# A streaming-encoder trunk on one core: SBUF places of matmul operands, and the piece size of the weight split

## Chip, cores and metric

The kernel runs on one core of a Trainium2 chip. The metric is device time in microseconds (us), the median of the runs. A second number, the span, is the time from the first to the last instruction in the one execution that was profiled.

## What is computed

Two identical layers are applied to 256 tokens of width 2048, all in float32. Biases, the rotary tables and the masks are left out here.

```python
def reference(x, ...):
    x = layer_norm(x, ln_in_g, ln_in_b)
    for l in range(DEPTH):                       # 2 layers
        h = x @ w_in[l]                          # 2048 -> 512 + 256 + 64 + 4 * 1024
        c_q, c_kv, k_rope, rq, rk, rv, rg = split_columns(h)
        a = mla_group(...)                       # 8 heads, softmax, low-rank q and kv
        r = retention_group(...)                 # 4 heads, decayed scores, group norm, gate
        mix = jnp.concatenate([a, r], axis=-1) @ w_out[l]           # 2048 -> 2048
        x = layer_norm(ALPHA * x + mix, ln1_g[l], ln1_b[l])
        f = (jax.nn.silu(x @ w_gate[l]) * (x @ w_up[l])) @ w_down[l]  # 2048 -> 5632 -> 2048
        x = layer_norm(ALPHA * x + f, ln2_g[l], ln2_b[l])
    return x
```

## The kernel before

**Numbers in two parts.** Each operand of a large matmul is held as two tiles of type float32r, a rounded part `hi` and the rest `lo`. The function `split` makes them: ScalarE casts the source into `hi` (line 250), and VectorE subtracts `hi` from the source into `lo` (line 251). A product takes three matmuls for each 128 rows of the contraction, called a triple below: hi by hi, hi by lo, lo by hi.

**Which operand is loaded and which is streamed.** TensorE loads 128 columns of one operand as its stationary operand (a weight load, PEld in the profile) and then streams the other one, the moving operand. There are two arrangements.
- `mm_x` (lines 238 to 240) and the function `mm` of the Strassen blocks (lines 804 to 806) load 128 tokens of the activations (`xTh`, `xTl`, `hTh`, `hTl`, `sfh`, `sfl`, `mixAh` and others) and stream 512 columns of the weights (320 in the block `ckv`).
- `mm_w` (lines 245 to 247) loads 128 columns of the weights and streams 256 tokens of the activations.

**Weights.** All weights lie in HBM as a stream of blocks, in the order of `PLAN` and `UNITS`. A block is at most 2048 columns on 128 partitions (1 MB). The class `Weights` walks through the stream. SP's queue loads a block into one of three `raw` buffers, up to three blocks ahead of the split. `_prep` splits one block into one of three `hi` and one of three `lo` buffers, and `done`, called after the last matmul on a block, frees its buffers and calls `_prep` for the block three places later. A plain block (kind "std") is split in two halves, so there are two casts and two subtractions. The blocks of the Strassen scheme (kinds B11, T1, B21, T2, T3, T4, B22) are split in one piece of 2048 columns already, some of them after VectorE has added two raw blocks (line 187).

**Amount of work for each layer.** There are 80 plain blocks of 4 by 512 columns that two token halves stream (24 matmuls each), 48 more matmuls of 512 columns in `pr` and `pv`, and ten Strassen chunks of 180 matmuls of 512 columns each. Of those 180, 48 load `sfh` or `sfl` (the outputs `sY`, `sZ` and part of `sW`); the others load `xTh` or `xTl`. `mm_w` has 1296 matmuls of 256 columns in a layer, and `ckv` has 96 of 320 columns.

**Order of work.** The order of instructions on each engine is fixed when the program is built. At the end of the attention part, and at the end of the feed-forward part of the first layer, `chunk_tail` keeps three weight blocks and finishes token half 0 before token half 1, so that the layer norm of half 0 (`Norm.apply`, lines 277 to 285, on VectorE, then transposes on TensorE and a split into `xTh` and `xTl`) runs beside the matmuls of half 1. `chunk_head` of the next part begins with half 0 in the same way. There are three such handovers. While they last, the splits of the next weight blocks and the layer norm share VectorE and ScalarE.

**Where the tiles lie.** SBUF is filled from the bottom by pools, one behind the other: `const`, `wraw`, `wspl`, `small`, and then `att` or the pools of the feed-forward part. Tiles begin at multiples of 32 bytes. Two unused tiles, `pad0` and `pad1`, and a third, `pad2`, shift what lies behind them. Modulo 256 bytes, in the program as built, the operands begin here (before the change):

```
res, xTh, xTl                                      128
raw, hi, lo                                        192
sfh, sfl                                           192
hTh, hTl                                           128
cqTh, cqTl, ckT, mixAh, mixAl, mixRh, mixRl        128
qT, kT, vt, rv (float32 attention operands)        128
ident                                               96
```

All steps inside these tiles from one operand of a matmul to the next are multiples of 256 bytes. So in `mm_x`, `mm` and `mm_w` the stationary and the moving operand stand at distance 64 modulo 256 (in one direction or the other), except for the matmuls on `sfh` and `sfl`, where the distance to `hi` and `lo` is 0. The distance is that of the addresses along the free dimension of a partition.

Of the kernel before, what the change touches and what calls it, by code (L numbers as in the profile page):

```python
# [10 lines left out]
F32 = mybir.dt.float32  # L11
# [7 lines left out]
P = 128  # L19
# [92 lines left out]
def trunk(ctx: ExitStack, tc: tile.TileContext, x, pos, w, lnp, cols, eye, consts, out):  # L112
# [3 lines left out]
    const = ctx.enter_context(tc.tile_pool(name="const", bufs=1))  # L116
    wraw = ctx.enter_context(tc.tile_pool(name="wraw", bufs=3))
    wspl = ctx.enter_context(tc.tile_pool(name="wspl", bufs=3))
    small = ctx.enter_context(tc.tile_pool(name="small", bufs=6))
    psp = ctx.enter_context(tc.tile_pool(name="psp", bufs=8, space=PSUM))  # L120

    res = const.tile([P, 2, D], F32, name="res")
    xTh = const.tile([P, KD, S], F32R, name="xTh")
    xTl = const.tile([P, KD, S], F32R, name="xTl")
# [5 lines left out]
    mhalf = const.tile([P, 8], F32, name="mhalf")  # L130

    ident = const.tile([P, P], F32, name="ident")
    const.tile([P, 88], F32, name="pad0")

    def bank(tag_name):
        return psp.tile([P, 512], F32, tag="ps", name=tag_name)
# [1 line left out]
    class Weights:  # L138
# [26 lines left out]
        def _prep(self):  # L165
            i = self.n_prep
            if i >= len(UNITS):
                return
            self.loads(i + 1)
            hi = wspl.tile([P, 2048], F32R, tag="hi", name=f"hi{i}")  # L170
            lo = wspl.tile([P, 2048], F32R, tag="lo", name=f"lo{i}")
            kind, b = UNITS[i]
            if kind == "std":
                n = SIZES[b]
                raw = self.raw.pop(b)
                for a, e in ((0, n // 2), (n // 2, n)):
                    split(hi[:, a:e], lo[:, a:e], raw[:, a:e])
            else:
                r = {j: self.raw.get(b[j]) for j in b}
                into, frm = {"B11": ("11", None), "B21": ("21", None), "B22": ("22", None), "T1": ("11", "12"),  # L180
                             "T2": ("11", "22"), "T4": ("11", "21"), "T3": ("12", "22")}[kind]
                if frm is not None:
                    if kind in STRASSEN_ADD_BY_DMA:
                        j = b[frm]
                        G.dma_start(r[into], w[OFFS[j]:OFFS[j + 1]].rearrange("(p n) -> p n", p=P), accum_op=ALU.add)
                    else:
                        V.tensor_tensor(r[into], r[into], r[frm], ALU.add)  # L187
                split(hi, lo, r[into])
                for j in {"T4": ("11", "21"), "T3": ("12",), "B22": ("22",)}.get(kind, ()):
                    self.raw.pop(b[j])  # L190
            self.hi[i], self.lo[i] = hi, lo
            self.n_prep += 1
            self.loads(i + 4)
# [55 lines left out]
    def split(hi, lo, src):  # L249
        A.copy(hi, src)  # L250
        V.tensor_tensor(lo, src, hi.bitcast(F32), ALU.subtract)  # L251
# [169 lines left out]
    for l in range(DEPTH):  # L421
# [317 lines left out]
        ffp = ff_ctx.enter_context(tc.tile_pool(name=f"ff{l}", bufs=1))  # L739
        W.rpool = ff_ctx.enter_context(tc.tile_pool(name=f"rs{l}", bufs=3))  # L740
        normf = Norm(f"f{l}")
        ffp.tile([P, 16], F32, tag="pad", name="pad1")
        sfh = ffp.tile([P, 4, 4, P], F32R, tag="sfh", name="sfh")
        sfl = ffp.tile([P, 4, 4, P], F32R, tag="sfl", name="sfl")

# [123 lines left out]
            hprev.append((0, c, v2))  # L869
            hprev.append((1, c, v5))  # L870

        ffp.tile([P, 48], F32, tag="pad2", name="pad2")
        for f0, f1 in FF_PARTS:
            nk = 4 * (f1 - f0)
            hTh = ffp.tile([P, 12, S], F32R, tag="hTh", name="hTh")
# [136 lines left out]
```

## Time and profile before

| what | us |
|---|---|
| median of 3 runs | 2206.98 |
| lowest and highest of them | 2205.0, 2208.04 |
| the profiled execution's own time | 2205.94 |
| its span | 2204.1 |
| TensorE busy | 2170.3 |
| VectorE busy | 1590.1 |
| ScalarE busy | 1024.4 |

The profiled execution is 1.04 us faster than the median. Its own time holds 1.84 us that lie outside the span. The granted clock of TensorE has a mean of 0.998 of full speed. The busy time of TensorE is a sum over instructions whose ends are modelled, so the pace of the matmuls is read from their starts.

### The profile page before, as it was taken

How to read it: one execution, taken by the hardware profiler on the slowest of the kernel's cores; microseconds unless marked ns; L12 is line 12 of the kernel's file. 1: busy time of each engine (PE TensorE's matmuls, PEld its weight loads, DVE VectorE, ACT ScalarE, POOL GpSimd, SP SyncE). 2: the span in 40 equal slices, each digit the busy share in tenths (PEclk: the TensorE clock that was granted, in tenths of full speed). 3: DMA queues.
4: the chain of work that ended last, by engine and by line, in shares of the span. 5: the costliest groups of instructions: out<-in, count | busy, mean ns of one | idle time of the engine just before them, and what ended most of it. 6: DMA issues, size and time to landing. Idle time of an engine off the chain costs nothing.

```text
span 2204.1 us, 26848 instructions
## 1 busy us (share of the span) xinstructions
PE 2170.3 (98%) x11084; PEld 1838.2 (83%) x11084; DVE 1590.1 (72%) x1687; ACT 1024.4 (46%) x1089; POOL 35.5 (2%) x46
## 2 busy tenths in 40 slices
PE   6999999999999999999999999999999999999997
PEld 5988988788888888888889899878888888888886
DVE  8565675887698578788675656667967885877976
ACT  4554333455455345455344543335544553545552
POOL 0000000000000000000000000000000000000000
PEclk9999999999999999999999999999999999999999
DMA  7544455566567557476555444555665674565653
GB/s 258 210 156 153 173 203 179 211 209 229 172 228 253 205 193 245 161 259 195 190 196 178 151 168 167 204 188 191 225 235 188 231 243 166 200 250 208 210 210 115
DMA packets 63467, 441.22 MB, mean 200 GB/s; under 512 B 7408, under 2 KB 7664, under 8 KB 11504
## 3 DMA queue, kind: packets, MB, share of 16 engines
q1 hardware_dynamic: 60048, 418.46, 52.0%
q0 software_dynamic: 2880, 20.97, 5.2%
q8 instruction: 87, 1.43, 0.3%
q14 instruction: 36, 0.29, 0.0%
q10 hardware_dynamic: 416, 0.07, 0.0%
HBM read 437.38 MB, written 2.10 MB: 199 GB/s over the span
## 4 chain that ended last, share of the span: by engine, by line
PE 48%; DVE 2%; issue 0%; ACT 0%; DVEq 0%; ACTq 0%
PE db L238 4%; PE db L240 4%; PE db L239 4%; PE sX L805 2%; PE sX L804 2%; PE sW L805 2%; PE sW L804 2%; PE sX L806 2%; PE sW L806 2%; PE prq L246 1%; PE prq L247 1%; PE prq L245 1%; PE sQ L805 1%; PE sQ L804 1%; PE sQ L806 1%; PE wo L239 1%
## 5 line engine op out<-in xcount | busy, mean ns | idle before, releaser
L251 DVE TENSOR_TENSOR lo<-raw,hi 128x1024 fp32r<-128x1024 f32 (+3 forms) x754 | 1033.5, 1407 | 418.9 <-ACT hi L250 417.0
L250 ACT CAST hi<-raw 128x1024 fp32r<-128x1024 f32 (+3 forms) x754 | 874.7, 1199 | 990.4 <-PE db L240 298.6
L238 PE MATMUL db<-hi,hTh 128*128 128x512 f32 x704 | 278.2, 395 | 0.0
L239 PE MATMUL db<-lo,hTh 128*128 128x512 f32 x704 | 275.3, 391 | 0.0
L240 PE MATMUL db<-hi,hTl 128*128 128x512 f32 x704 | 272.6, 391 | 0.0
L238 PEld LDWEIGHTS db<-hi,hTh 128*128 128x128 f32 x704 | 132.2, 188 | 31.0 <-ACT hTh L250 3.7
L240 PEld LDWEIGHTS db<-hi,hTl 128*128 128x128 f32 x704 | 132.1, 188 | 30.3
L239 PEld LDWEIGHTS db<-lo,hTh 128*128 128x128 f32 x704 | 132.3, 188 | 27.4
L245 PE MATMUL prq<-xTh,hi 128*128 128x256 f32 x512 | 144.0, 281 | 0.0
L246 PE MATMUL prq<-xTl,hi 128*128 128x256 f32 x512 | 142.6, 279 | 0.0
L247 PE MATMUL prq<-xTh,lo 128*128 128x256 f32 x512 | 142.6, 279 | 0.0
L187 DVE TENSOR_TENSOR raw<-raw,raw 128x2048 f32<-128x2048 f32 x60 | 137.1, 2285 | 0.5
L805 PE MATMUL sX<-lo,xTh 128*128 128x512 f32 x320 | 125.9, 394 | 0.0
L804 PE MATMUL sX<-hi,xTh 128*128 128x512 f32 x320 | 125.5, 392 | 0.0
L806 PE MATMUL sX<-hi,xTl 128*128 128x512 f32 x320 | 124.5, 389 | 0.0
L245 PEld LDWEIGHTS prq<-xTh,hi 128*128 128x128 f32 x512 | 97.2, 190 | 0.1
L246 PEld LDWEIGHTS prq<-xTl,hi 128*128 128x128 f32 x512 | 96.2, 188 | 0.1
L247 PEld LDWEIGHTS prq<-xTh,lo 128*128 128x128 f32 x512 | 96.1, 188 | 0.0
L805 PE MATMUL sQ<-lo,xTh 128*128 128x512 f32 x240 | 94.5, 394 | 0.0
L804 PE MATMUL sQ<-hi,xTh 128*128 128x512 f32 x240 | 94.1, 392 | 0.0
L806 PE MATMUL sQ<-hi,xTl 128*128 128x512 f32 x240 | 93.2, 388 | 0.0
L691 DVE SCALAR_TENSOR_TENSOR res<-res,db 128x512 f32<-128x512 f32 x64 | 43.8, 684 | 67.7 <-PE db L240 67.7
(265 smaller groups left out, 3974.7 us busy)
## 6 DMA issues: line engine op xcount, KB each, us to landing
raw<-w SPq DMA_DIRECT2D x377, 1024.0 KB, 4.9
raw<-w POOLq DMA_DIRECT2D x20, 1024.0 KB, 8.4
raw<-w SPq DMA_DIRECT2D x8, 640.0 KB, 3.9
lng<-lnp SPq DMA_DIRECT2D x4, 1024.0 KB, 4.9
lnb<-lnp SPq DMA_DIRECT2D x4, 1024.0 KB, 5.8
res<-x SPq DMA_DIRECT2D x4, 512.0 KB, 6.4
out<-res SPq DMA_DIRECT2D x8, 256.0 KB, 2.6
cst<-consts SPq DMA_DIRECT2D x2, 976.5 KB, 8.2
```

The source lines that it names most:

```text
L187: V.tensor_tensor(r[into], r[into], r[frm], ALU.add)
L238: PE.matmul(ps[:, :ncol], sh, wh[:, k, :ncol], start=first and k == 0, stop=False)
L239: PE.matmul(ps[:, :ncol], sh, wl[:, k, :ncol], start=False, stop=False)
L240: PE.matmul(ps[:, :ncol], sl, wh[:, k, :ncol], start=False, stop=last and k == nk - 1)
L245: PE.matmul(ps_ap, wh[:, k, c0:c0 + P], xh[:, k, :], start=k == 0, stop=False)
L246: PE.matmul(ps_ap, wh[:, k, c0:c0 + P], xl[:, k, :], start=False, stop=False)
L247: PE.matmul(ps_ap, wl[:, k, c0:c0 + P], xh[:, k, :], start=False, stop=k == nk - 1)
L250: A.copy(hi, src)
L251: V.tensor_tensor(lo, src, hi.bitcast(F32), ALU.subtract)
L804: PE.matmul(ps, a, wh[:, k, :], start=first and k == 0, stop=False, skip_group_check=True)
L805: PE.matmul(ps, a, wl[:, k, :], start=False, stop=False, skip_group_check=True)
L806: PE.matmul(ps, b, wh[:, k, :], start=False, stop=k == 3, skip_group_check=True)
```

## The change

Two things are changed. `pad0` shrinks by 16 float32 elements (64 bytes), and an unused tile of 64 bytes is placed first in `small`; `pad1` and `pad2` go. With that `raw`, `hi` and `lo` move 64 bytes down, to 128 modulo 256. The pools behind `small` begin where they began. `sfh` and `sfl` move to 128, and `hTh` and `hTl` move by 256 bytes, which leaves them at 128. All operands of the large matmuls are then at distance 0 modulo 256. (Modulo 512 the distance to `hi` is 0 for `xTh`, `xTl`, `sfh`, `sfl`, `hTh` and `hTl`, and 256 for the attention tiles such as `mixAh`.)

Plain weight blocks from the fifth on are split in one piece, so that there is one cast and one subtraction of up to 2048 columns in place of two of up to 1024.

```diff
     small = ctx.enter_context(tc.tile_pool(name="small", bufs=6))
     psp = ctx.enter_context(tc.tile_pool(name="psp", bufs=8, space=PSUM))
 
+    small.tile([P, 16], F32, tag="pad", bufs=1, name="pad1")
     res = const.tile([P, 2, D], F32, name="res")
...
     ident = const.tile([P, P], F32, name="ident")
-    const.tile([P, 88], F32, name="pad0")
+    const.tile([P, 72], F32, name="pad0")
...
             if kind == "std":
                 n = SIZES[b]
                 raw = self.raw.pop(b)
-                for a, e in ((0, n // 2), (n // 2, n)):
+                for a, e in ((0, n // 2), (n // 2, n)) if i < 4 else ((0, n),):
                     split(hi[:, a:e], lo[:, a:e], raw[:, a:e])
...
         normf = Norm(f"f{l}")
-        ffp.tile([P, 16], F32, tag="pad", name="pad1")
         sfh = ffp.tile([P, 4, 4, P], F32R, tag="sfh", name="sfh")
...
-        ffp.tile([P, 48], F32, tag="pad2", name="pad2")
         for f0, f1 in FF_PARTS:
```

## Rows read from the trace of the kernel before

**Rows 1.** The page, part 1: busy time, share of the span, instructions of an engine.
```profile
PE 2170.3 (98%) x11084; PEld 1838.2 (83%) x11084; DVE 1590.1 (72%) x1687; ACT 1024.4 (46%) x1089; POOL 35.5 (2%) x46
```

**Rows 2.** Who PE waited for: us in total, times, longest.
```profile
PE ptx L282 <- DVE res L278: 17.2, 7, 11.5
```

**Rows 3.** Busy time by stretch (PE, PEld, DVE, ACT, POOL): first layer's feed-forward part.
```profile
410.00:1098.00 688.00, 688.00 (x3064) 565.25 (x3063) 522.58 (x425) 341.10 (x306) 8.90 (x10) 1.00 0.63 214
```

**Rows 4.** Groups by line and form, PE: busy us, mean ns of one, idle before.
```profile
L805 PE MATMUL sX<-lo,xTh 128*128 128x512 f32 x320 | 125.9, 394 | 0.0
L804 PE MATMUL sX<-hi,xTh 128*128 128x512 f32 x320 | 125.5, 392 | 0.0
L806 PE MATMUL sX<-hi,xTl 128*128 128x512 f32 x320 | 124.5, 389 | 0.0
...
L804 PE MATMUL sY<-hi,sfh 128*128 128x512 f32 x80 | 31.1, 389 | 0.0
```

**Rows 5.** Timeline of PE, 1008 to 1015 us: start, length; 12 steps between the rows.
```profile
1008.76 0.39 PE L804 MATMUL sX<-hi,xTh 128*128 128x512 f32 x1
...
1011.51 0.39 PE L804 MATMUL sY<-hi,sfh 128*128 128x512 f32 x1
...
1014.23 0.39 PE L804 MATMUL sX<-hi,xTh 128*128 128x512 f32 x1
```

**Rows 6.** Timeline of PE, first and last of 48 matmuls on two weight blocks.
```profile
1293.70 0.28 PE L245 MATMUL prq<-xTh,hi 128*128 128x256 f32 x1
...
1299.03 0.28 PE L247 MATMUL prq<-xTh,lo 128*128 128x256 f32 x1
...
1327.86 0.28 PE L245 MATMUL prq<-xTh,hi 128*128 128x256 f32 x1
...
1333.40 0.28 PE L247 MATMUL prq<-xTh,lo 128*128 128x256 f32 x1
```

**Rows 7.** Groups by line and form, PE, `mm_w` into `prq`.
```profile
L246 PE MATMUL prq<-xTl,hi 128*128 128x256 f32 x512 | 142.6, 279 | 0.0
```

**Rows 8.** Groups by line and form, DVE and ACT: the two sizes of the split.
```profile
L251 DVE TENSOR_TENSOR lo<-raw,hi 128x1024 fp32r<-128x1024 f32 x594 | 700.7, 1220 | 313.5 <-ACT hi L250 313.1
L250 ACT CAST hi<-raw 128x1024 fp32r<-128x1024 f32 x594 | 594.9, 1049 | 737.4 <-PE db L240 256.4 <-PE prq L246 109.0 <-issue 85.3
L251 DVE TENSOR_TENSOR lo<-raw,hi 128x2048 fp32r<-128x2048 f32 x140 | 320.2, 2287 | 96.0 <-ACT hi L250 94.6
...
L250 ACT CAST hi<-raw 128x2048 fp32r<-128x2048 f32 x140 | 267.3, 1909 | 242.2 <-DVE raw L187 100.1 <-PE db L240 42.2 <-PE sW L806 32.7
```

**Rows 9.** Timelines of DVE, ACT and PE at the second handover, 1098 to 1120 us.
```profile
1103.86 2.00 ACT L250 CAST hi<-raw 128x1024 fp32r<-128x1024 f32 x2 [0.79 <-PE db L240]
1105.18 2.35 DVE L251 TENSOR_TENSOR lo<-raw,hi 128x1024 fp32r<-128x1024 f32 x2
...
1107.05 2.00 ACT L250 CAST hi<-raw 128x1024 fp32r<-128x1024 f32 x2 [0.71 <-PE db L240]
1107.44 0.69 DVE L251 TENSOR_TENSOR xTl<-ptx,xTh 128x512 fp32r<-128x512 f32 x1
1108.13 2.36 DVE L251 TENSOR_TENSOR lo<-raw,hi 128x1024 fp32r<-128x1024 f32 x2
1110.41 0.68 DVE L691 SCALAR_TENSOR_TENSOR res<-res,db 128x512 f32<-128x512 f32 x1
...
1113.06 0.66 PE L282 MATMUL ptx<-ident,res 128*128 128x128 f32 x4 [0.56 <-DVE res L278]
```

**Rows 10.** Timelines of DVE and PE behind that handover, 1123 to 1128 us.
```profile
1124.24 2.36 DVE L251 TENSOR_TENSOR lo<-raw,hi 128x1024 fp32r<-128x1024 f32 x2 [1.17 <-ACT hi L250]
1126.52 0.68 DVE L251 TENSOR_TENSOR xTl<-ptx,xTh 128x512 fp32r<-128x512 f32 x1
...
1127.29 0.47 PE L240 MATMUL cq<-hi,xTl 128*128 128x512 f32 x1
```

**Rows 11.** Timeline of DVE in a Strassen chunk; the first of the three is block T2.
```profile
1009.10 4.56 DVE L251 TENSOR_TENSOR lo<-raw,hi 128x2048 fp32r<-128x2048 f32 x3 [0.83 <-ACT hi L250]
```

## The prediction

> **What bounds the kernel now.** I read the page's busy times first. TensorE is busy for 98% of the span and VectorE for 72% [rows 1]. A busy share of matmuls says little, so the list of who waited comes next. TensorE's longest entry is 17.2 us, of which 11.5 are one wait at the start [rows 2]; the rest of that entry is 5.7 us in six waits. In the first feed-forward part, which is a third of the span, TensorE works for 688.00 of 688.00 us [rows 3]. TensorE therefore bounds the kernel. Two things can move the time: the pace of the matmuls while they follow each other, and the few places where TensorE waits. VectorE and ScalarE count only at those places.
>
> The pace is read from starts. Twelve matmuls into `sX` take from 1008.76 to 1011.51, 2.75 us or 229.2 ns a step. The next twelve, into `sY`, take from 1011.51 to 1014.23, 2.72 us or 226.7 ns [rows 5]. Both stream 512 columns of the same kind of `hi` and `lo` buffer and load 128 columns. What differs is the place of the loaded tile: `xTh` and `xTl` stand at distance 64 from the streamed one, `sfh` and `sfl` at 0. The groups over the whole run agree. The three matmuls of a triple have means of 392, 394 and 389 ns on `sX`, and 389 in each of the three groups on `sY` (one of them stands in the rows) [rows 4]. The lengths are modelled, but they move with the steps. A triple is thus 7.5 ns longer at distance 64 by the starts, and 8 by the means, each with a rounding of a few ns. I take 7.
>
> **Part one, the places.** *512 columns.* A layer has 80 * 24 + 48 + 10 * 180 = 3768 such matmuls, two layers have 7536. Of them 2 * 10 * 48 = 960 load `sfh` or `sfl` and stand at 0 already. 6576 remain, or 2192 triples; at 7 ns each that is 15.3 us. The lower end is nothing, if distance isn't the reason. The upper end, at 8 ns, is 17.5 us. A smaller bound lies between: the attention tiles come to 256 modulo 512, where no operand here is that the trace can be asked about. That concerns `wo`, `pr` and `pv`, 864 matmuls or 288 triples, 2.0 us. At distance 64 these tiles and `xTh` run alike, although they differ modulo 512, so I leave them in.
>
> *256 columns with the weights as the loaded operand.* Here distance 64 shows two paces, at the same addresses modulo 256. One block takes from 1293.70 to 1299.03 for 47 steps, 113.4 ns each. Another takes from 1327.86 to 1333.40, 117.9 ns [rows 6]. Worked out from first and last start of each, 19 of the 54 blocks keep the fast pace throughout, and the mean step of the undisturbed triples of all 54 is 115.7. The group's mean length of 279 ns [rows 7], less the 162.3 that lie between length and step on `sY` (389 less 226.7), gives 116.7 with the waits in it, which fits. There are 2592 of these matmuls. If all come to the fast pace the gain is 2.3 * 2592 = 6.0 us; if all fall to the slow one, the loss is 2.2 * 2592 = 5.7. No row shows this arrangement at distance 0. 113.4 ns for 256 columns is half of 226.7 for 512, which is the pace at distance 0, so I take that as the pace without disturbance, and 6.0 us.
>
> *320 columns.* 64 triples at 7 ns would be 0.4 us. I take nothing.
>
> *A rule that speaks against this part.* The rows say that two sets of matmuls, alike but for the loaded tile's place, differ by 7 ns a triple [rows 4, 5]. The Trainium skill, page "TensorE: Matmul & The Clock Gate", section "Part 2: What happens when you issue a matmul", says that the streamed operand and the weight load have independent read ports into SBUF and that loading the next weights takes no bandwidth from the running matmul. By that rule the distance is worth nothing, and the sum would hold part two alone. The trace of this kernel doesn't agree with it as it stands.
>
> **Part two, one piece.** A cast of 2048 columns takes 1909 ns against two of 1049, a subtraction 2287 against two of 1220 [rows 8]. 594 halves are 297 blocks; three of them (the second to the fourth) stay in halves. So ScalarE is spared 294 * 189 ns = 56 us and VectorE 294 * 153 ns = 45 us. TensorE waits for neither in the stretches where they run side by side [rows 3], so I cost this at nothing there. What the change adds is a delay. VectorE could begin when the first half was cast, 1.05 us after the cast's start; now it begins after 1.91, that is 0.86 us later where it is idle, and its end comes about 0.7 us later.
>
> Between the handovers two finished blocks lie ahead of TensorE, some 5 to 10 us of matmuls. The tightest block there is T2 of a Strassen chunk. Its subtraction begins at 1009.10 and takes 2.29, so it ends at 1011.39 [rows 11], and TensorE begins at 1011.51 [rows 5]. But T2 is split in one piece before and after, and what leads up to it doesn't change. TensorE arrives some 0.03 us earlier there (four triples at 7 ns) in 20 chunks, 0.6 us at most. I leave it out.
>
> At a handover it is different, because VectorE works without a break and TensorE ends up waiting for it. Take the second. The next block's cast begins at 1103.86, VectorE is free for its subtraction at 1105.18 [rows 9]. In one piece the cast ends at 1105.77, and the subtraction then ends at 1108.1 instead of 1107.5. `xTl` follows, ending at 1108.8. The third cast begins at 1107.05 and ends at 1108.96; its subtraction ends at 1111.3 instead of 1110.5. Behind it on VectorE stands the residual of token half 1 (1110.41), then its statistics and its norm, and for that norm TensorE waits until 1113.06 [rows 9]. So that wait grows by 0.8 us. Once more behind it: a subtraction that began on a first half at 1124.24 has `xTl` behind it (1126.52), and the matmul at 1127.29 needs that piece as soon as it ends [rows 10]. One piece ends 0.7 us later, and so does this. That is 1.5 us for a handover and 4.5 us for three. Below, it is nothing, if another order of instructions or TensorE's spare matmuls cover it. Above, each of four blocks at a handover loses its 0.86 us: 10.3 us.
>
> **Sum.** On the profiled execution: 2205.94 - 15.3 - 6.0 + 4.5 = 2189.1. The median of the runs is 1.04 us above the profiled execution, so 2190.2; I predict 2190.
>
> **Rivals.**
> *The blocks of `mm_w` don't come to the fast pace.* For it: both paces exist at one distance [rows 6], so something besides the distance chooses between them. Against it: `sY` keeps one pace in all its groups [rows 4]. If the mix stays: 2190 + 6 = 2196. If all are slow: 2190 + 11.7 = 2202.
> *The place of the loaded tile, not the distance, sets the pace, or neither does.* `sfh` and `sfl` are also the only loaded activation tiles that begin at 192 modulo 256; the others begin at 128. The rows on the activations can't tell the two apart. After the change all begin at 128. The 320 triples on `sfh` and `sfl` would then lose 7 ns each, 2.2 us, nothing would be won, and part two decides: 2206.98 + 2.2 + 4.5 = 2214, or 2211 if the places do nothing at all. Against it: in `mm_w` the loaded tiles begin at 192 too, and the slow pace exists there [rows 6]. It decides as soon as `sX` stays at 392, 394 and 389.
> *One piece starves TensorE in the Strassen chunks.* VectorE is busy for 522.58 of 688 us in that part [rows 3], and in the chunks themselves still denser. A loss of 0.8 us in each of 20 chunks would cost 16 us and bring the time to 2206, no change. Against it: each chunk has four plain blocks, which save 0.15 us of VectorE each, and T2's chain doesn't hold one of them.
> *Nothing is lost at the handovers:* 2190 - 4.5 = 2185.5.
>
> **Chances.** The forecast 0.57; `mm_w` stays mixed or slow 0.18; the place or nothing 0.13; Strassen chunks starve 0.07; no loss at the handovers 0.05. A change of 0.2% (4.4 us) is about what a measurement of this kernel can tell from none. The forecast, the fifth case and nearly all of the second are faster by more than that, which makes 0.79. Half of the fourth and a little of the second and third are within it: 0.07. The rest of the third and fourth is slower: 0.14. The likeliest case's own range goes from 2184 (no loss at the handovers, 8 ns a triple) to 2198 (10.3 us lost there, attention tiles left out). The range from 2184 to 2204 takes in the second case and leaves out the third and most of the fourth.
>
> **What the profile after would show.** `sX`, `db` and `wo` at 389 ns in all three matmuls of a triple, 2.72 us for twelve. `prq` and `pg` at 276 to 277 ns. 434 subtractions of 2048 columns and six of 1024. At each handover, the wait of `ptx` for VectorE longer by 0.8 us. The prediction is wrong if `sX` keeps its 394, or if `sY` rises to it.

## The result and the profile after

| | median us | lowest to highest | runs |
|---|---|---|---|
| before | 2206.28 | 2205.0 to 2208.04 | 4 |
| after | 2223.02 | 2220.9 to 2224.24 | 4 |

The ratio is 1.0074, with a 95% interval from 1.0057 to 1.0092. The change costs about 17 us where a gain of 17 was forecast. The profiled execution after took 2223.0 us, its span is 2221.2 us, 17.1 more than before.

The busy times (page of after, part 1: busy us, share of the span, instructions) answer to [rows 1]:

```profile
PE 2181.8 (98%) x11084; PEld 1844.7 (83%) x11084; DVE 1569.2 (71%) x1385; ACT 996.8 (45%) x787; POOL 35.5 (2%) x46
```

TensorE has the same share, so it still sets the time. VectorE fell by 20.9 us and ScalarE by 27.6, to no use. (Both have 302 instructions fewer: 294 blocks of 2048 columns and the eight of `ckv`, which have 1280.)

Groups by line and form of after (busy us, mean ns of one, idle before and its releaser) answer to [rows 4, 7, 8]:

```profile
L246 PE MATMUL prq<-xTh,hi 128*128 128x256 f32 x512 | 146.0, 285 | 0.0
L248 PE MATMUL prq<-xTh,lo 128*128 128x256 f32 x512 | 145.1, 283 | 0.0
L247 PE MATMUL prq<-xTl,hi 128*128 128x256 f32 x512 | 144.8, 283 | 0.0
L805 PE MATMUL sX<-lo,xTh 128*128 128x512 f32 x320 | 125.4, 392 | 0.8 <-DVE lo L252 0.4
L806 PE MATMUL sX<-hi,xTl 128*128 128x512 f32 x320 | 124.7, 390 | 0.0
L804 PE MATMUL sX<-hi,xTh 128*128 128x512 f32 x320 | 124.6, 389 | 0.0
...
L805 PE MATMUL sY<-lo,sfh 128*128 128x512 f32 x80 | 32.1, 401 | 1.5 <-DVE lo L252 1.5
...
L252 DVE TENSOR_TENSOR lo<-raw,hi 128x2048 fp32r<-128x2048 f32 x434 | 989.9, 2289 | 490.2 <-ACT hi L251 488.7
```

Three things are to be seen. `sX` has come down from 392 to 394 to 389, except where a wait shows. `prq` has gone up, from 279 to 283 on the line shown in [rows 7]. And two groups now have idle time before them that VectorE's `lo` ended, `sX` and `sY`, which had none.

The pace from starts, one undisturbed stretch of `prq` (timeline of TensorE, first and last of the rows of line 246, 72 steps apart), answers to [rows 6]:

```profile
1303.05 0.28 PE L246 MATMUL prq<-xTh,hi 128*128 128x256 f32 x1
...
1311.69 0.28 PE L246 MATMUL prq<-xTh,hi 128*128 128x256 f32 x1
```

That is 8.64 us, 120.0 ns a step: slower than both paces of before (113.4 and 117.9).

The waits of after, first of the matmuls themselves, which answers to [rows 2], then of the weight loads (us in total, times, longest):

```profile
PE ptx L283 <- DVE res L279: 20.9, 7, 14.5
PE sY L805 <- DVE lo L252: 1.5, 8, 0.2
...
PEld sW L804 <- DVE v L846: 6.2, 17, 0.5
...
PEld sY L805 <- DVE lo L252: 4.8, 8, 0.6
PEld sX L805 <- DVE lo L252: 4.2, 8, 0.7
...
PEld sQ L805 <- DVE lo L252: 2.7, 8, 0.3
```

The list for the matmuls shows little, because it is the weight load ahead of the matmul that waits. None of the four entries of the weight loads is in the same list of before. Of the 20.9 us on `ptx`, 14.5 are the start; the other six waits are 6.4 us, against 5.7 before.

What a wait costs is read from starts again. T2's first triple in one chunk (timeline of TensorE, after):

```profile
657.43 0.39 PE L806 MATMUL sX<-hi,xTl 128*128 128x512 f32 x1
657.65 0.39 PE L804 MATMUL sY<-hi,sfh 128*128 128x512 f32 x1
658.24 0.50 PE L805 MATMUL sY<-lo,sfh 128*128 128x512 f32 x1 [0.20 <-DVE lo L252]
658.58 0.40 PE L806 MATMUL sY<-hi,sfl 128*128 128x512 f32 x1
658.82 0.40 PE L804 MATMUL sY<-hi,sfh 128*128 128x512 f32 x1
```

The row says 0.20 us. The step into it is 585 to 590 ns, against 227, and the step behind it 340. That is 0.47 us lost. (`sX`, `sY`, `sQ`, `sW` and `sR` name the PSUM banks that the matmuls of a chunk add into.) Summed over the run in this way, `sY`, `sX`, `sQ` and `sW` lose 13.3 us at these places, where before loses nothing; the list of the matmuls gives 1.9 for them.

**The account.** I sorted all steps between matmul starts by columns, and into steps at pace (up to 245 ns for 512 columns, 130 for 256) and long ones (waits, and the steps around other instructions). Sums in us; "over" means over 226.67 ns for 512 columns and 113.33 for 256.

| | before | after | difference |
|---|---|---|---|
| start of the first matmul | 11.5 | 14.45 | +2.9 |
| 512 columns at pace, over | 15.95 | 4.35 | -11.6 |
| 256 columns at pace, over | 6.1 | 17.0 | +10.9 |
| 512 columns, long steps, over | 24.9 | 40.0 | +15.1 |
| sum | | | +17.3 |

The span differs by 17.1. The late start comes from a DMA: VectorE's first step on data waits for the token positions until 9.38 us, where before it waited until 6.44 (timelines of VectorE, before and after).

```profile
6.44 0.17 DVE L403 CAST pf<-pb 128x2 f32<-128x2 int32 x1 [5.00 <-DMA pb<-pos]
```

```profile
9.38 0.17 DVE L404 CAST pf<-pb 128x2 f32<-128x2 int32 x1 [7.94 <-DMA pb<-pos]
```

Another run of the same kernel, told below, starts at 11.6, so the 2.9 us are chance and not the change.

### The profile page after: what moved, and what is told of

Its sections match the earlier page's. It is cut to its first block, busy times and chain, and to the rows that moved or that the text cites. A ratio compares the mean times of both kernels' runs of the same rounds, so it can differ in the third digit from the quotient of the medians.

```text
span 2221.2 us, 26234 instructions
## 1 busy us (share of the span) xinstructions
PE 2181.8 (98%) x11084; PEld 1844.7 (83%) x11084; DVE 1569.2 (71%) x1385; ACT 996.8 (45%) x787; POOL 35.5 (2%) x46
## 5 line engine op out<-in xcount | busy, mean ns | idle before, releaser
L252 DVE TENSOR_TENSOR lo<-raw,hi 128x2048 fp32r<-128x2048 f32 (+2 forms) x452 | 1011.6, 2246 | 501.5 <-ACT hi L251 500.0
L251 ACT CAST hi<-raw 128x2048 fp32r<-128x2048 f32 (+2 forms) x452 | 846.6, 1878 | 955.3 <-PE db L241 301.8
```

## The experiments

Short names: **places** for the shifted tiles, **piece** for the split in one piece. Ratios are to before on the same chip.

**1. The two parts, each alone.** `e1_places_only` has the four lines of the diff that move tiles and the halves of before. `e2_piece_only` has the places of before and this change of a line:

```diff
-                for a, e in ((0, n // 2), (n // 2, n)):
+                for a, e in ((0, n // 2), (n // 2, n)) if i < 4 else ((0, n),):
```

> The tiles moved as in the change, the split still in halves; the order of instructions on every engine is that of the kernel before. Theory A (two causes that add: the places set the pace of the matmuls, the one piece makes TensorE wait): matmuls of 512 columns step at 226.7 ns, those of 256 at 120.0, TensorE's waits stay as before; -11.6 and +10.9 us on 2206.3, so about 2205.6, and up to 2.9 more if the late start belongs to the places. Theory B (the waits come from the places as well): the waits of 15 us are here, about 2221.

> The split in one piece from the fifth block on, all tiles where they were before. Theory A: the pace is that of before (687 ns for a triple of 512 columns, a mean step of 115.7 for 256 columns), and TensorE waits 15 us more, nearly all of it for a lo in the Strassen chunks; 2221, up to 2224 if the late start comes back. Theory B: 2206.

Measured: places alone 2205.53 us against 2205.62, ratio 1.000 (0.999 to 1.001). Piece alone 2219.66, ratio 1.0063 (1.0048 to 1.0078). Theory A came, so the waits are not the places'. Thus the whole loss is the piece's, but the places are not without effect. Groups by line and form of `e1_places_only`:

```profile
L239 PE MATMUL db<-hi,hTh 128*128 128x512 f32 x704 | 275.9, 392 | 0.0
L240 PE MATMUL db<-lo,hTh 128*128 128x512 f32 x704 | 274.0, 389 | 0.0
L241 PE MATMUL db<-hi,hTl 128*128 128x512 f32 x704 | 271.5, 389 | 0.0
L246 PE MATMUL prq<-xTh,hi 128*128 128x256 f32 x512 | 146.2, 286 | 0.0
```

In the account, 512 columns at pace win 12.3 us and 256 columns at pace lose 10.9; the long steps are as before (25.3 against 24.9). Two effects cancel. With the piece alone the long steps rise by 11.9 us, not by the 15 expected; the loss of 512 columns over the floor stays (16.96, 1.0 more than before), and that of 256 columns rises by 0.9, to which part 3 comes back.

**2. Other distances.** Five kernels in halves, which differ from `e1_places_only` in the two pads alone, so that `raw`, `hi` and `lo` stand at another distance from the activations. For 128:

```diff
-    small.tile([P, 16], F32, tag="pad", bufs=1, name="pad1")
+    small.tile([P, 48], F32, tag="pad", bufs=1, name="pad1")
...
-    const.tile([P, 72], F32, name="pad0")
+    const.tile([P, 40], F32, name="pad0")
```

> Halves, and hi and lo at distance 128 modulo 256 from all activations. Theory A with a fixed cost of a weight load (13.3 ns = 226.7 - 512/2.4 = 120.0 - 256/2.4): the same two paces as at distance 0, about 2206. Rival: distance 0 is one of several places, and at 128 the loads disturb less (113.4 ns for all of 256 columns, about 2184 with 226.7) or more (118 and 229 or above, over 2206).

> Halves, and hi and lo 64 bytes below the activations modulo 256, not above. If the direction matters, the two arrangements change roles: matmuls of 512 columns show two paces, those of 256 one. If only the size of the distance matters, all is as before: 687 ns for a triple of 512, two paces at 256, about 2206.

> Halves, hi and lo 32 bytes above the activations modulo 256. If a load has a fixed cost of 13.3 ns wherever it doesn't meet the stream, and 64 is a place with some meetings: 226.7 ns for 512 columns, and for 256 between 113.4 and 120; 2184 to 2206. If small distances meet more: above 229, over 2210.

> Halves, hi and lo 32 bytes below the activations modulo 256. If the direction decides, as 192 (699 ns a triple) against 64 (687) says, this lies above distance 0: 512 columns between 680 and 699 ns a triple, 256 columns about 118 ns; 2206 to 2240.

> Halves, hi and lo 96 bytes above the activations modulo 256. So far the triples of 512 columns took 680 at 0, 687 at 64, 690 to 705 at 128, 700 at 32, 192 and 224. If 64 is a place of its own, 96 is like 32: about 700, 2240 to 2245. If distances from 64 to 128 get slowly worse: 687 to 697, 2206 to 2240.

The distance in the table is the way from the activations up to `hi` and `lo`. In `mm_x` and `mm` that is from the loaded operand to the streamed one, in `mm_w` from the streamed one to the loaded one.

| distance modulo 256 | us (runs) | triple of 512 columns, ns | mean step of 256 columns, ns |
|---|---|---|---|
| 0 | 2205.53 (10) | 680 | 120.0 |
| 32 | 2244.61 (1) | 700 | 118.3 |
| 64 (before) | 2205.62 (13) | 687, on `sfh` and `sfl` 680 | 115.7 |
| 96 | 2244.01 (1) | 700 | 118.0 |
| 128 | 2241.24 (1) | 690 to 706 | 119.0 |
| 192 | 2243.77 (1) | 700 | 117.6 |
| 224 | 2240.47 (1) | 700 | 116.8 |

The five other distances have one run each, but they lie 34 us or more above distance 0, far outside the spread of before. In `e7_d032` the groups by line and form show that `sY`, at distance 0 before, has risen with `sX`:

```profile
L804 PE MATMUL sX<-hi,xTh 128*128 128x512 f32 x320 | 126.4, 395 | 0.0
...
L804 PE MATMUL sY<-hi,sfh 128*128 128x512 f32 x80 | 31.6, 395 | 0.0
```

So the distance does set the pace of 512 columns. The place of one operand alone doesn't: before, `hi` at 192 gave 680 ns with `sfh` at 192 and 687 with `xTh` at 128, and `xTh` at the same 128 comes to 680 with `hi` at 128. The pace is no smooth function of the distance: 0 is best, 64 is next, and the others tried cost 18 to 20 ns a triple in the mean. For 256 columns the order is another one, with 64 the best and 0 the worst. 320 columns don't answer to the distance: their step has a mean of 146.6 to 146.7 ns in all seven. Of the expectations, "like 32" for 96 came, and so did the rivals that wanted more disturbance at 32 and at 128. At 192 neither theory held, and at 224 I had 512 columns between 680 and 699 and got 700.

**3. Where the piece costs.** `e5_piece_not_strassen` takes one piece everywhere but in the plain blocks of the Strassen chunks, `e6_piece_strassen_only` only there (80 blocks):

```diff
-                for a, e in ((0, n // 2), (n // 2, n)):
+                for a, e in ((0, n),) if (PLAN[b][0] in ("w_gate", "w_up") and PLAN[b][4] > 0) else ((0, n // 2), (n // 2, n)):
```

> Tiles where they were before. One piece for the plain blocks outside the Strassen chunks alone; the four plain blocks of each chunk stay in halves. Theory A1 (the waits come from the one-piece blocks inside the chunks): 2206 to 2209, what is left being the handovers and the values of the attention. Theory A2 (any plain block in one piece costs its share): the chunks hold 80 of the 294 blocks, so some 10 of the 14 us stay, 2216.

> Tiles where they were before. One piece for the 80 plain blocks inside the Strassen chunks alone. Theory A1: nearly all of the 14 us, 2217 to 2220. Theory A2: 4 of the 14 us, 2210.

Measured: 2208.55 against 2206.42, ratio 1.0009 (1.0000 to 1.0019), and 2219.15, ratio 1.0057 (1.0041 to 1.0074). Theory A1 came. The chunks alone cost 12.7 us; all other blocks together cost 2.1, at the edge of what can be told from none. Read from starts, 9.8 of the 12.7 are the waits at `sX`, `sY`, `sQ` and `sW`. Another 1.1 are steps of 512 columns at pace, in `sW`, `sY` and other outputs of the chunks, and 1.3 are steps of 256 columns, which lie in the attention and not in the chunks. Neither the places nor TensorE's order decide which of these blocks go at the fast pace: the fourth to the tenth of the 54 have a step of 113.3 ns in before and of 117.8 in `e14_su_t4` (below), where both are those of before. What decides it is not shown, and the 1.3 us are not put down to a cause here. In the other blocks of `e5_piece_not_strassen` the long steps rise by 2.3 us: about 1.1 at the attention values (`prv` and `po`) and 1.2 at eight steps of `db`, the product with `w_down`. The waits of `ptx` behind the start don't grow (16.9 us less 11.6, against 17.2 less 11.5).

**4. Why the chunks are slower.** The program as built shows that the places leave the order of instructions on every engine as it was. The piece does not: 903 of 10937 positions in TensorE's order differ, and VectorE's order in a chunk is another. The order is made by the builder, the program that turns the kernel into each engine's instructions, and with casts of another length it comes out another. A chunk takes its weight blocks in the order B11, sg2, T1, B21, T2, sg3, T3, T4, su2, B22, su3; sg2 and sg3 are its two plain gate blocks, su2 and su3 its two plain up blocks, the others belong to the Strassen scheme. VectorE before, in a chunk (timeline; the first row holds T2 and the two halves of sg3):

```profile
646.92 4.56 DVE L251 TENSOR_TENSOR lo<-raw,hi 128x2048 fp32r<-128x2048 f32 x3 [0.83 <-ACT hi L250]
651.40 2.28 DVE L187 TENSOR_TENSOR raw<-raw,raw 128x2048 f32<-128x2048 f32 x1
653.60 2.28 DVE L251 TENSOR_TENSOR lo<-raw,hi 128x2048 fp32r<-128x2048 f32 x1
655.81 0.68 DVE L833 TENSOR_TENSOR v<-sY,v 128x512 f32<-128x512 f32 x1
656.41 2.28 DVE L251 TENSOR_TENSOR lo<-raw,hi 128x2048 fp32r<-128x2048 f32 x1
```

The same chunk after (the first row holds T2, sg3 and T3):

```profile
655.89 6.69 DVE L252 TENSOR_TENSOR lo<-raw,hi 128x2048 fp32r<-128x2048 f32 x3 [0.84 <-ACT hi L251]
662.50 0.68 DVE L833 TENSOR_TENSOR v<-sY,v 128x512 f32<-128x512 f32 x1
663.11 2.28 DVE L188 TENSOR_TENSOR raw<-raw,raw 128x2048 f32<-128x2048 f32 x1
667.42 4.50 DVE L252 TENSOR_TENSOR lo<-raw,hi 128x2048 fp32r<-128x2048 f32 x2 [2.03 <-ACT hi L251]
```

Line 187 (188 after) is the sum for T4. It stood 4.5 us behind the start of T2's subtraction, ahead of T3; now it stands 7.2 us behind it. T4's cast has to wait for it, and VectorE idles for 2.03 us until T4 can be subtracted. TensorE then waits for T4's `lo` (`sQ`), and for the `sW` bank, which VectorE empties later (`v<-sW`, line 846). In the program as built the sum stands behind T3's subtraction in eight of the 20 chunks of the kernel after, and the waits at `sQ` and `sY` and all but one of the long ones at `sW` lie in these eight. To test this, `e9_t4_add_early` keeps the one piece of `e6_piece_strassen_only` and writes T4's sum ahead of T3's split:

```diff
-                if frm is not None:
+                if frm is not None and kind != "T4":
...
+                if kind == "T3":
+                    V.tensor_tensor(r["11"], r["11"], r["21"], ALU.add)
                 split(hi, lo, r[into])
```

> As the sixth run (one piece inside the Strassen chunks alone, tiles as before), but the sum for T4 is written in the program ahead of T3's split, as the built order of the kernel before had it on VectorE. Theory C (TensorE waits because the one piece made the builder put T4's sum behind T3's subtraction): the 12.7 us fall to 3 or less, 2206 to 2210. Theory D (the longer pieces themselves come too late, in any order): 2216 to 2220.

Measured: 2212.31 us against 2207.07, ratio 1.0023 (1.0014 to 1.0032). The loss fell from 12.7 to 5.2 us, more than half of the way, but not to the 3 or less that theory C wanted; theory D's 2216 to 2220 did not come. So the place of T4's sum is a cause, and not the only one. The waits of the weight loads, first of `e6_piece_strassen_only`:

```profile
PEld sW L804 <- DVE v L846: 5.1, 16, 0.5
...
PEld sX L805 <- DVE lo L251: 3.9, 8, 0.6
...
PEld sY L805 <- DVE lo L251: 3.3, 8, 0.4
...
PEld sQ L805 <- DVE lo L251: 2.7, 8, 0.3
```

then of `e9_t4_add_early`:

```profile
PEld sX L807 <- DVE lo L253: 3.8, 8, 0.6
...
PEld sY L807 <- DVE lo L253: 3.4, 8, 0.4
...
PEld sW L806 <- DVE v L848: 1.3, 8, 0.2
```

`sQ` is gone and `sW` is down to a quarter, as this cause wants; from starts the two lost 5.0 us, and now lose nothing. `sX` (the block sg3) and `sY` (T2) stay, in eight chunks each, and not the same eight. From starts they lose 2.6 and 2.2 us, 4.8 of the 5.2.

**5. The rest: which blocks.** With the early sum, `e13_sg_t4` takes only the two gate blocks of a chunk in one piece (`PLAN[b][0] == "w_gate"` in the condition), `e14_su_t4` only the two up blocks (`"w_up"`).

> T4's sum is written ahead of T3's split, and of the four plain blocks of a Strassen chunk only the two gate blocks are taken in one piece (40 blocks); the places are those of before. With all four in one piece and the same early sum the kernel was 5.2 us slower than before. First theory: a later subtraction of the block itself costs this; the gate piece sg3 delays its own first triple, the up pieces delay T2 of the next chunk. Then the loss is shared: about 2 to 3 us here and as much with the up blocks alone. Second theory: what is left of the changed order costs it; here 192 positions of TensorE's order differ from before, with the up blocks none. Then this run loses nearly all of it, about 5 us, and the other none. Third theory: the up piece that stands ahead of T2 costs it all; then this run is equal to before.

> As the run beside it, but only the two up blocks of a Strassen chunk are taken in one piece (40 blocks); TensorE's order of instructions is that of before. First theory (each piece delays what stands behind it): about 2 to 3 us slower than before. Second theory (the changed order of TensorE): equal to before within 1 us. Third theory (the up piece ahead of T2): about 5 us slower, with the waits at the first triple on T2's lo.

Measured: 2209.73 us against 2205.55, ratio 1.0018 (1.0009 to 1.0028), and 2206.64, ratio 1.0005 (0.9995 to 1.0014). The loss lies with the gate blocks: of the three theories the second comes nearest, 4.2 us and 1.1 that can't be told from none. By the waits it is not the whole story: of the 4.2 us, 2.6 are at `sX`, and the 2.2 us that `sY` lost in `e9_t4_add_early` are in neither run. The waits of the weight loads of `e13_sg_t4` hold `sX` and neither `sY` nor `sW` for VectorE:

```profile
PEld sX L807 <- DVE lo L253: 3.8, 8, 0.6
```

In `e14_su_t4` none of the three is there but one `sW` of 0.3 us. The two waits have different causes.

*`sX`.* VectorE in `e13_sg_t4`, in a chunk with this wait (the first row is T2, the third holds sg3 and T3):

```profile
606.43 2.29 DVE L253 TENSOR_TENSOR lo<-raw,hi 128x2048 fp32r<-128x2048 f32 x1 [1.43 <-ACT hi L252]
608.76 2.29 DVE L189 TENSOR_TENSOR raw<-raw,raw 128x2048 f32<-128x2048 f32 x1
610.97 4.49 DVE L253 TENSOR_TENSOR lo<-raw,hi 128x2048 fp32r<-128x2048 f32 x2
```

Line 189 is T4's sum again, now ahead of sg3's subtraction, which so ends at 613.2; the matmul on it starts at 613.31, after a step of about 400 ns in place of 227. In the program as built this order is found in exactly eight of the 20 chunks of `e13_sg_t4`, of `e9_t4_add_early` and of the kernel after, and in none of before or of `e14_su_t4`; the eight waits at `sX` lie in these eight chunks. In the other twelve chunks of `e13_sg_t4` sg3 is in one piece as well, but T4's sum stands behind it, and there is no wait. So the length alone doesn't do it; the order is what goes with the wait. That the order alone would do it, with sg3 in halves, was not run.

*`sY`.* This wait appears only with the gate and the up blocks in one piece together. In `e9_t4_add_early` VectorE's order from sg2 to T2 is that of `e14_su_t4` in those eight chunks. What differs is sg2's one piece. Measured from the same step of TensorE (the first on `lo` into `sW`), T2's subtraction begins 2.84 us later before, 2.87 in `e14_su_t4` and 3.30 in `e9_t4_add_early`: 0.43 us are passed on through VectorE's chain of work from sg2 to T2. Before, T2's subtraction ended 0.34 us ahead of the first matmul on it in the mean of these eight chunks, so 0.43 is enough for a wait. This is a reading of the timelines; no run isolates it.

**6. Two places.** The distances above say that the two kinds of matmul want different places. `e10_two_places` keeps the halves, puts `hi` and `lo` at distance 0, and shifts them by 64 bytes for the blocks of `mm_w` alone (`OFF_W` is 16 elements, and `by_w` tells these blocks). The room comes from `small`, which gets two buffers in place of six.

```diff
-    small = ctx.enter_context(tc.tile_pool(name="small", bufs=6))
+    small = ctx.enter_context(tc.tile_pool(name="small", bufs=2))
+    small.tile([P, 48], F32, tag="pad", bufs=1, name="pad1")
...
-    const.tile([P, 88], F32, name="pad0")
+    const.tile([P, 8], F32, name="pad0")
...
-            hi = wspl.tile([P, 2048], F32R, tag="hi", name=f"hi{i}")
-            lo = wspl.tile([P, 2048], F32R, tag="lo", name=f"lo{i}")
+            o = OFF_W if kind == "std" and by_w(b) else 0
+            hi = wspl.tile([P, 2112], F32R, tag="hi", name=f"hi{i}")[:, o:o + 2048]
+            lo = wspl.tile([P, 2112], F32R, tag="lo", name=f"lo{i}")[:, o:o + 2048]
```

> Halves, the tiles as in the change, but the hi and lo of blocks that mm_w loads are placed 64 bytes further up, in buffers 256 bytes longer (the small tiles give up the room: two buffers for each in place of six). If the pace follows from the distance of the load and the stream alone: 512 columns at distance 0 keep 226.7 ns, 256 columns at distance 64 fall back from 120.0 to a mean of 115.7; 2205.5 - 11 = 2194.5, between 2192 and 2197. If the pace hangs on the place of the buffers instead: 120 stays, 2205.

Measured: 2195.38 us (2193.32 to 2196.56) against 2207.07, ratio 0.9947 (0.9934 to 0.9959). 2194.5 was expected from the distance alone. It beats both kernels, the kernel before by 11.7 us and the one after, measured beside another run of before, by about 28. In the program as built the order on TensorE, VectorE, ScalarE and SP is that of `e1_places_only`, so the fewer small buffers did not change it. Groups by line and form:

```profile
L255 PE MATMUL prq<-xTh,hi 128*128 128x256 f32 x512 | 143.8, 281 | 0.0
L256 PE MATMUL prq<-xTl,hi 128*128 128x256 f32 x512 | 142.4, 278 | 0.0
...
L815 PE MATMUL sX<-hi,xTl 128*128 128x512 f32 x320 | 124.5, 389 | 0.0
```

`sX` has the pace of after and `prq` that of before: in the account 512 columns at pace are 3.55 us over the floor, and the mean step of 256 columns is 115.8 ns. The buffers are an odd multiple of 256 bytes long here, so two thirds of the matmuls on `xTh` and `xTl` stand at 256 modulo 512 from `hi`, and the pace of 512 columns is that of `e1_places_only` even so.

**7. After once more.** `e12_after_again` is the kernel after, unchanged, for its start and its waits.

> The changed kernel once more, for its start. In its first profile the token positions landed 8.2 us after their issue and TensorE began at 14.45 us, against 5.2 and 11.5 in the kernel before and 11.3 to 11.7 in the eight runs since. If that is the transfer's chance: 11.3 to 11.8 and about 2220. If it belongs to the changed kernel: 14 to 15 and 2223.

Measured: 2221.42 us in one run. The waits of the matmuls begin with

```profile
PE ptx L283 <- DVE res L279: 16.6, 7, 11.6
```

The first matmul starts at 11.6 us and the long steps are 40.9 us, as in the first profile (40.0). The waits are the change's, the late start is not.

## Why the prediction was wrong, point by point

Two steps failed above all: the pace of 256 columns, and the price of nothing for the one piece in the Strassen chunks. Neither of the two signs that I named for being wrong came (`sX` did fall to 389 where nothing waits, and `sY` rose to 401 only on the line with the wait). Of the other things that I expected to see, `prq` at 283 in place of 276 to 277 was the one that told.

**512 columns: right, the size 3 us too large.** All three matmuls of a triple are at 389 on `sX`, as forecast, and the rival "the place or nothing" falls with the other distances, where `sY` rises to 395. The term was 15.3 us; measured alone it is 12.3. Twelve steps had given 7.5 ns a triple; over all undisturbed triples on `xTh` the means are 686.9 before and 680.1 with the places alone. Some 0.7 us go the other way, on `sfh` (680.1 to 682.4), and the remaining 1.9 are triples that did not win in full: by output the gain at pace is 6.7 to 7.0 ns a triple on `sX`, `sQ`, `sR` and the `xTh` part of `sW`, 6.3 on `db`, 5.3 on `wo`, 3.6 on `prv` and 3.0 to 3.3 on `cq`, `gb` and `ub`. In the last ones many triples have a long step in them; why that takes the gain away is not shown. The attention tiles, at 256 modulo 512, run at 227 ns as the others do.

**256 columns: the step that failed first.** "113.4 ns for 256 columns is half of 226.7 for 512, which is the pace at distance 0, so I take that as the pace without disturbance." At distance 0 the step is 120.0 ns. That 113.4 is half of 226.7 was a coincidence: at distance 0, 512 columns take 226.7, 320 take 146.7 and 256 take 120.0, which is the time of the columns at 2.4 GHz (the granted clock has a mean of 0.997 of that) and 13.3 ns more in each case. A sum with a fixed part doesn't halve with the columns. -6.0 us were forecast, +10.9 came, and even the upper bound of 5.7, taken from the slow pace of before, was too low: a bound from one distance doesn't hold for another.

**The rule that spoke against part one.** Two runs that differ in the pads alone have triples of 680 and 700 ns. The Trainium skill, page "TensorE: Matmul & The Clock Gate", section "Part 2: What happens when you issue a matmul", has it that weight loads and the streamed operand read through independent ports. The traces don't agree with what that rule would give here, no effect of the distance. They don't show what the two share.

**One piece: the step that failed most.** "TensorE waits for neither in the stretches where they run side by side, so I cost this at nothing there", and of T2: "what leads up to it doesn't change". The prediction held VectorE's order in a chunk for fixed. The chunks lost 12.7 us by `e6_piece_strassen_only`. The piece changed what leads up to T2, sg3 and T4, since the order was built anew around casts of another length. The early sum gave 7.5 us back by the medians. Of the other 5.2, 2.6 us go with T4's sum ahead of sg3, and 2.2 with the longer sg2 ahead of T2, the latter by a reading of timelines. The margin at T2 was misread as well: TensorE needs its `lo` one step later than the 1011.51 that I took, so there were 0.35 us, not 0.12. The rival "one piece starves TensorE in the Strassen chunks" had 16 us and a chance of 0.07. It was the case; its place and nearly its size were right, its reason (0.8 us in every chunk) was not, since nearly all waits come in two groups of eight chunks, and most of the loss goes with the order.

**The saved time of the engines was too large, too.** I took 153 ns a block on VectorE and 189 on ScalarE, from two means of single instructions. Two halves in a row take less than twice one of them: in one row of the timeline they take 2.36 us against 2.28 for one piece, and 2.00 against 1.91 [rows 9]. 294 blocks at 0.07 to 0.09 are 21 and 26 us, which is what the busy times show.

**The handovers: 4.5 us forecast, 2.1 us for all blocks outside the chunks, and no longer waits of `ptx` there.** After has, at the second handover (timeline of TensorE):

```profile
1122.89 0.66 PE L283 MATMUL ptx<-ident,res 128*128 128x128 f32 x4 [0.36 <-DVE res L279]
```

The wait is 0.36 us against 0.56 in [rows 9], not 0.8 more. VectorE's order is another one here, too: the residual of token half 1, which stood behind the third subtraction, now stands ahead of it (timeline of VectorE, after):

```profile
1118.70 0.68 DVE L692 SCALAR_TENSOR_TENSOR res<-res,db 128x512 f32<-128x512 f32 x1
1119.30 2.28 DVE L252 TENSOR_TENSOR lo<-raw,hi 128x2048 fp32r<-128x2048 f32 x1
```

That was the lower bound of this term ("another order of instructions").

**The sum.** On the profiled execution the terms were -11.6 for 512 columns (-15.3 forecast), +10.9 for 256 columns (-6.0), +15.1 for the long steps (+4.5) and +2.9 by chance for the start. The long steps of the whole change rise by 15.1 us where the piece alone has 11.9; the waits at `sX`, `sY`, `sQ` and `sW` are 13.3 against 10.0. I read this so: a TensorE that is faster by the places comes earlier to the same subtraction, and part of what the pace gives goes into the wait. No run isolates it. The two parts alone, -0.1 and +14.0 us, make 13.9 where the whole change costs 16.7 (12.6 to 20.3 by its interval), so the medians show no more than a sum.

## What to carry to other kernels

Ask of every edit that changes an instruction's length whether the order of instructions is rebuilt around it, and compare the orders on each engine before costing the edit at nothing; here one sum that moved behind one subtraction made 7.5 of the 12.7 us that the chunks lost. A pace read for one shape is not scaled to another: measure each shape at each placement, and expect two shapes to want different placements. Read the waits of the weight loads and the steps between starts along with TensorE's own list of waits, which showed 1.9 of 13.3 us.

## What the runs showed of the hardware

- The step between float32r matmuls of 512 columns depends on the distance of the loaded and the streamed operand modulo 256 bytes: a triple takes 680 ns at 0, 687 at 64, 700 at 32, 96, 192 and 224, and 690 to 706 at 128. Whether the distance was 0 or 256 modulo 512 made no difference that could be seen, and neither did 64 or 320.
- At distance 0 a step is the columns at 2.4 GHz plus 13.3 ns for 512, 320 and 256 columns. At 64, 256 columns go at 113.4 ns in some blocks, faster than that, and at 117.9 in others; which blocks are the fast ones differs between two runs with the same places and the same order on TensorE, and the mean is 115.7 before and 115.8 in `e10_two_places`. 320 columns take 146.6 to 146.7 at every distance tried.
- A wait costs TensorE more than the wait: in the kernel after, the step behind a late weight load took 334 to 341 ns in place of 227 in 33 cases, at each of the four kinds of waits, and 293 to 299 in the eight others, all at `sW`.
